# Hybrid conformer and state-space block on one core: time steps inside the exponentials, depthwise taps inside the scan, lower halves of the scan's weights by adding loads

## The chip, the core and the metric

The kernel runs on one NeuronCore of a Trainium2 chip. The metric is the device time of one execution in microseconds; the median of several runs counts. The engines are named as in the profile: PE (TensorE, matmuls), ACT (ScalarE), DVE (VectorE), POOL (GpSimd) and SP (SyncE, here only a queue for loads).

## The reference

One block on x of 512 tokens by 1024 channels, in float32:

```python
h = rms_norm(x, g);  proj = h @ w_in             # u_glu, z, xbc, dt_raw, gates
v = val * sigmoid(gt)                            # conformer branch
v = causal depthwise conv of 31 taps(v);  conv_out = silu(layer_norm(v)) @ pw_w + pw_b
xbc = silu(causal conv of 4 taps(xbc))           # state-space branch: xs, B, C
dt = softplus(dt_raw + dt_bias);  a_cs = cumsum(dt * -exp(a_log)) in each chunk
xdt = x * dt
y_diag = (C B^T * exp(a_cs[l] - a_cs[s]), causal) @ xdt
states = B^T @ (exp(a_cs[-1] - a_cs) * xdt);  carried from chunk to chunk
y = y_diag + exp(a_cs) * C @ prev + x * d_skip
ssm_out = grouped_rms_norm(y * silu(z)) * norm_g @ out_w
x = x + rms_norm((g_conv * conv_out + g_ssm * ssm_out) @ w_out)
x = x + rms_norm(silu-gated FFN(rms_norm(x)))    # hidden size 2816
```

The branch has 32 heads of 64 in 8 groups, with a state of 128 in each group. The kernel uses chunks of 128 tokens, so there are four.

## The kernel before

Every large product is made three times with operands in two halves: an operand is split into an upper half (`hi`, a cast to fp32r) and a lower half (`lo`, what the cast left out), and `mm3` (L241 to L252) issues hi by hi, hi by lo and lo by hi into one PSUM bank. PE therefore carries a dense row of matmuls from end to end, and everything else has to keep ahead of it.

The weights come in pieces of 128 x 1024 in a fixed list (`ORDER`, L147 on), numbered n. SP loads a piece into `raw` (L194), ACT casts it to `whi` (L202), and then there are two ways to the lower half. DVE subtracts `whi` from `raw` (L209); or ACT writes -whi into `wlo` (L206) and POOL issues a load of the same piece that adds to it (L207, an adding load). Before the change, in `w_part` (L195 to L211), pieces with an odd number above 8 and ahead of the `gc` gates go the second way, and even ones go to DVE. Five pieces have buffers at a time, and a piece is split up to three (`zz`: four) pieces ahead of its use, as soon as PE is done with the piece that had the buffer.

The stages are: the GLU projections (`val`, `glu`, pieces 0 to 18), with z of group 0 and dt in between; then the scan, groups 0 to 7 (pieces 19 to 76); then the gates `gs`, the last strips of the scan's output product and the gates `gc`; then the pointwise product, w_out and the FFN.

A group g of the scan projects x (two strips), B and C. Each strip is 24 matmuls into one bank, followed by a causal convolution of 4 taps (`conv4`, L596: one pass on ACT, three on DVE, a silu on ACT). Odd groups from 3 on also multiply an earlier pair of groups with the output weights (`so`), and even groups from 2 on project z for two groups at once (`zz`, four pieces that are used together, L634). In between stand the steps of the group before: `s1` (L656) transposes x, B and makes C B^T; `s2` (L689) makes the states (pS) and y_diag (yd); `s3` (L712) the part from the carried state (pY) and the norm; `s4` (L752) transposes y back. In `s1`, DVE reads each bank of transposed x twice, for `xdt` (times dt) and for `y` (times d_skip), and makes `xdec` out of xdt. `make_L` (L482) loads the running sums of a group to all partitions, masks them on POOL and takes 16 exponentials on ACT with `nacs` (minus the sums) as bias; DVE then multiplies L by C B^T (L686).

The 31-tap convolution of the conformer branch is 8 strips of one ACT pass and 30 DVE taps (L507 to L518). `conv_some` hands out taps in a fixed number: 12 per strip in the GLU stage, `TAPS[g]` in group g, `TAPS_GATE` behind each gate.

The order of instructions on each engine is fixed when the program is built: a scheduler places each instruction, in program order as far as its inputs are ready by its own estimates. Activations passed to `by_table` (L476) keep their order among each other, so that the activation table changes seldom.

Of the kernel before, what the change touches and what calls it, by code (L numbers as in the profile page):

```python
# [10 lines left out]
F32 = mybir.dt.float32  # L11
F32R = mybir.dt.float32r
BF16 = mybir.dt.bfloat16
AF = mybir.ActivationFunctionType
ALU = mybir.AluOpType
# [3 lines left out]
P = 128  # L19
T = 512  # L20
NT = T // P
# [4 lines left out]
HD = 64  # L26
G = 8
HG = H // G
# [49 lines left out]
LOAD_AT = {0: 0, 1: 1, 2: 2, 3: 4, 5: 6}  # L78
RAW_AHEAD = 3
EARLY_U = 4  # L80
DMA_EVERY = 2
DMA_FROM = 8
ADD_LO = (2, 3) + tuple(range(7, FF // P, 2))
GU_AHEAD = 5
# [1 line left out]
S_AHEAD = 5  # L86

TAPS_GLU = 12
TAPS = (6, 14, 18, 20, 20, 20, 20, 20)
TAPS_GATE = 5  # L90
ADD_S1 = (3, 5)
ORDER_DVE = (
# [72 lines left out]
def b3(ap, n):  # L165

    return ap.unsqueeze(len(ap.shape)).to_broadcast(list(ap.shape) + [n])
# [3 lines left out]
def block_kernel(ctx: ExitStack, tc: tile.TileContext, x, xT, x0, prm, hp, gp, wf, w, out):  # L171
    nc = tc.nc
    act, dve, pe, pool = nc.scalar, nc.vector, nc.tensor, nc.gpsimd
# [11 lines left out]
    seq = {key: n for n, key in enumerate(ORDER)}  # L185
# [10 lines left out]
    def w_part(n, c, by_dve=False):  # L196
        hi, lo = split[n]
        src = first_raw[n, c.start] if n < 3 else raws[n][:, c]
        if by_dve:
            dve.tensor_copy(hi[:, c], src)  # L200
        else:
            mark[n, c.start] = act.copy(hi[:, c], src)  # L202
        after_zz = n > 5 and ORDER[n - 2] in ZZ_LAST
        every = n % DMA_EVERY == DMA_EVERY - 1 and DMA_FROM < n < seq[("gc", 0)] and not after_zz
        if every or 0 <= n - seq[("wo", 0)] < ADD_WO:
            act.activation(lo[:, c], hi[:, c].bitcast(F32), AF.Copy, scale=-1.0)  # L206
            mark["lo"] = pool.dma_start(lo[:, c], w[n][:, c].bitcast(F32R), accum_op=ALU.add)  # L207
        else:
            mark["wlo"] = dve.tensor_tensor(out=lo[:, c], in0=src, in1=hi[:, c].bitcast(F32), op=ALU.subtract)  # L209
            if ORDER[n] == ZZ_LAST[0]:  # L210
                not_before(noted["yz_1"], mark["wlo"])  # L211
# [84 lines left out]
    ssd = br.enter_context(tc.tile_pool(name="ssd", bufs=1))  # L296
# [24 lines left out]
    def flat(a):  # L321
        return a.rearrange("p a b -> p (a b)")
# [9 lines left out]
    ps = aux_tile("warm_ps")  # L332
# [27 lines left out]
    hp_t = ssd.tile([P, 3, H], F32, name="hp_t")  # L360
# [97 lines left out]
    def running_sums():  # L458
        pcs = aux_tile("pcs")
        pe.matmul(pcs[:, :CH], tri, flat(ta), start=True, stop=True)  # L460
        act.copy(flat(acs), pcs[:, :CH])
        pend = aux_tile("pend")
        pe.matmul(pend[:, :CH], ones, flat(ta), start=True, stop=True)
        act.activation(flat(cd), pend[:, :CH], AF.Exp)
        act.activation(flat(eacs), flat(acs), AF.Exp)
        dve.tensor_tensor(out=flat(tb), in0=pend[:, :CH], in1=flat(acs), op=ALU.subtract)
        act.activation(flat(dec), flat(tb), AF.Exp)
        dve.tensor_scalar(out=flat(nacs), in0=flat(acs), scalar1=-1.0, scalar2=None, op0=ALU.mult)
        pT = aux_tile("pT")
        pe.transpose(pT[:, :P], flat(acs), ident)  # L470
        act.copy(acsT, pT[:, :P])
        for c in range(NT):
            nc.scalar.dma_start(scr[:, c, :], acsT[c * H : (c + 1) * H, :])


    def by_table(ins):  # L476

        if "table" in mark:
            not_before(ins, mark["table"])
        mark["table"] = ins  # L480
# [69 lines left out]
    for j in range(NK):  # L550
# [3 lines left out]
        if j == DT2:  # L554
            running_sums()
            L = {0: make_L(0)}
# [99 lines left out]
    def s1(g):  # L656
        s = st[g]
        hs = slice(HG * g, HG * (g + 1))
        xdt = ssd.tile([P, NT, HG, HD], F32, tag="xdt", name=f"xdt{g}")
        y = ssd.tile([P, NT, HG, HD], F32, tag="y", bufs=2, name=f"y{g}")  # L660
        xdec = ssd.tile([P, NT - 1, HG, HD], F32, tag="xdec", name=f"xdec{g}")
        for c2 in range(2):
            ps = aux_tile(f"pxT{g}_{c2}")
            for c in range(2):
                tok = slice((2 * c2 + c) * P, (2 * c2 + c + 1) * P)
                for e in range(2):
                    pe.transpose(ps[:, c * GW + e * P : c * GW + (e + 1) * P], s[f"x{e}"][:, tok], ident)
            cs = slice(2 * c2, 2 * c2 + 2)
            pv = ps.rearrange("p (c h d) -> p c h d", c=2, h=HG)
            dve.tensor_tensor(out=xdt[:, cs], in0=pv, in1=b3(dtt[:, cs, hs], HD), op=ALU.mult)  # L670
            dve.tensor_tensor(
                out=y[:, cs], in0=pv,
                in1=b3(hp_t[:, 2:3, hs].to_broadcast([P, 2, HG]), HD), op=ALU.mult,
            )
        dve.tensor_tensor(out=xdec, in0=xdt[:, : NT - 1], in1=b3(dec[:, : NT - 1, hs], HD), op=ALU.mult)
        ps = yd_tile(0, f"pBT{g}")
        for c in range(NT - 1):
            pe.transpose(ps[:, c * P : (c + 1) * P], s["B"][:, c * P : (c + 1) * P], ident)
        BT = ssd.tile([P, NT - 1, P], F32, tag="BT", name=f"BT{g}")
        act.copy(flat(BT), ps[:, : (NT - 1) * P])  # L680
        ps = yd_tile(1, f"pcb{g}")
        for c in range(NT):
            tok = slice(c * P, (c + 1) * P)
            pe.matmul(ps[:, tok], s["B"][:, tok], s["C"][:, tok], start=True, stop=True)
        L = s["L"].rearrange("p h c l -> p h (c l)")
        dve.tensor_tensor(out=L, in0=L, in1=ps.unsqueeze(1).to_broadcast([P, HG, T]), op=ALU.mult)  # L686
        s.update(xdt=xdt, y=y, xdec=xdec, BT=BT)

    def s2(g):  # L689
        s = st[g]  # L690
        hs = slice(HG * g, HG * (g + 1))
        prev = ssd.tile([P, NT - 1, HG, HD], F32, tag="prev", name=f"prev{g}")
        tmp = ssd.tile([P, HG, HD], F32, tag="ptmp", bufs=2, name=f"ptmp{g}")
        pa, pb = aux_tile(f"pSa{g}"), aux_tile(f"pSb{g}")
        pS = [pa[:, :GW], pa[:, GW:], pb[:, :GW]]
        for c in range(NT - 1):
            pe.matmul(pS[c], s["BT"][:, c, :], s["xdec"][:, c].rearrange("p h d -> p (h d)"), start=True, stop=True)
        act.copy(prev[:, 0].rearrange("p h d -> p (h d)"), pS[0])
        for c in range(1, NT - 1):
            dve.tensor_tensor(out=tmp, in0=prev[:, c - 1], in1=b3(cd[:, c, hs], HD), op=ALU.mult)  # L700
            dve.tensor_tensor(
                out=prev[:, c], in0=pS[c].rearrange("p (h d) -> p h d", h=HG), in1=tmp, op=ALU.add
            )
        yd = [yd_tile(n, f"yd{g}_{n}").rearrange("p (c h d) -> p c h d", c=2, h=HG) for n in range(2)]
        for c in range(NT):
            for h in range(HG):
                for i in range(0, P, HD):
                    half = slice(i, i + HD)
                    pe.matmul(yd[c // 2][half, c % 2, h, :], s["L"][:, h, c, half], s["xdt"][:, c, h, :], start=True, stop=True)
        s.update(prev=prev, yd=yd)  # L710

    def s3(g):  # L712
# [1090 lines left out]
```

## Time and profile before

| What | Value |
|---|---|
| median of 3 runs | 1017.67 us (1017.04 to 1017.77) |
| span of the profiled execution, first to last instruction | 1016.0 us |
| rest of the median around that span | 1.7 us |
| busy: PE, DVE, ACT, POOL | 1007.7, 847.9, 616.9, 106.7 us |
| moved by DMA | 155.02 MB |

The profile is of one execution and gives its span; the runs are timed apart from it, so the span is set beside their median. Busy time is summed by engine; a matmul's end is modelled, so that matmuls overlap in it, and short waits show better in the distances of their starts. In a group's line stand the source line, engine, operation, output and inputs, shapes and count, then busy time, the mean of one in ns, and the idle time ahead of it with what ended it. An arrow "<-" in brackets in a timeline names what a waiting instruction waited for.

### The profile page before, as it was taken

To read this page: it belongs to the slowest core of one execution; us is meant where nothing else is said; L and a number is where in the kernel's file an instruction comes from. 1 tells how busy PE (TensorE), PEld (TensorE's weight loads), DVE (VectorE), ACT (ScalarE), POOL (GpSimd) and SP (SyncE) were. 2 spreads that over 40 slices of the span, in tenths; PEclk is the share of its full clock that TensorE was granted. 3 is DMA by queue.
4 is the path that set the end of the run, shared out by engine and by line. 5 is a ranking of instruction groups with operands and counts; after the bars stand their busy time and mean duration, and the time that the engine had idled before them with its cause. 6 is when DMAs were issued, how large, how long until landed. Compare 5 with 4: busy or idle time off the path is not lost.

```text
span 1016.0 us, 15943 instructions
## 1 busy us (share of the span) xinstructions
PE 1007.7 (99%) x6184; PEld 881.7 (87%) x6184; DVE 847.9 (83%) x1233; ACT 616.9 (61%) x1038; POOL 106.7 (11%) x138
## 2 busy tenths in 40 slices
PE   9999999999999999999999999999999999999997
PEld 7898889888888888888888889889999999998886
DVE  7899977868696879678987889788999887899974
ACT  7655775667666746573552685466666566568552
POOL 0101202120121011100110111012000000001001
PEclk9999999999999999999999999999999999999999
DMA  8567635645554465356452355624755555469622
GB/s 302 151 168 218 158 96 145 187 110 144 158 151 117 130 182 151 102 135 163 99 139 69 114 142 165 223 104 118 230 151 160 153 143 146 128 177 295 212 83 83
DMA packets 43803, 155.02 MB, mean 153 GB/s; under 512 B 5072, under 2 KB 6096, under 8 KB 42704
## 3 DMA queue, kind: packets, MB, share of 16 engines
q1 hardware_dynamic: 30672, 105.44, 30.7%
q0 software_dynamic: 11136, 43.00, 21.7%
q10 hardware_dynamic: 1920, 5.57, 1.6%
q8 instruction: 48, 0.79, 0.3%
q14 instruction: 27, 0.22, 0.1%
HBM read 149.73 MB, written 4.26 MB: 152 GB/s over the span
## 4 chain that ended last, share of the span: by engine, by line
PE 87%; DVE 8%; ACT 3%; issue 1%; DMA 1%; SPq 0%; POOL 0%; POOLq 0%; DVEq 0%; ACTq 0%
PE xy L246 4%; PE xy L252 4%; PE xy L248 4%; PE pso L246 3%; PE pso L248 3%; PE pso L252 3%; PE yv L246 2%; PE yv L252 2%; PE yv L248 2%; PE px L246 2%; PE px L252 2%; PE px L248 2%; DVE a L514 2%; PE pz L248 2%; PE pz L252 2%; PE pz L246 2%
## 5 line engine op out<-in xcount | busy, mean ns | idle before, releaser
L514 DVE SCALAR_TENSOR_TENSOR a<-v,prm_t,a 128x511 f32<-128x511 f32 (+15 forms) x240 | 183.8, 769 | 14.3 <-ACT a L511 12.3
L202 ACT CAST whi<-raw 128x1024 fp32r<-128x1024 f32 x99 | 102.6, 1048 | 127.9 <-PE pso L248 36.7
L209 DVE TENSOR_TENSOR wlo<-raw,whi 128x1024 fp32r<-128x1024 f32 x58 | 70.6, 1220 | 32.7 <-ACT whi L202 32.5
L207 POOL DMA_DIRECT2D wlo<-in_w x41 | 36.5, 891 | 369.1 <-ACT wlo L206 171.4
L248 PE MATMUL pz<-wlo,hhi 128*128 128x512 f32 (+2 forms) x160 | 56.2, 351 | 0.2
L252 PE MATMUL pz<-whi,hlo 128*128 128x512 f32 (+2 forms) x160 | 56.1, 352 | 0.0
L246 PE MATMUL pz<-whi,hhi 128*128 128x512 f32 (+2 forms) x160 | 55.4, 353 | 0.0
L246 PE MATMUL px<-hhi,whi 128*128 128x512 f32 x128 | 50.2, 392 | 0.0
L246 PE MATMUL pso<-yh,whi 128*128 128x512 f32 x128 | 50.2, 394 | 0.0
L252 PE MATMUL px<-hhi,wlo 128*128 128x512 f32 x128 | 49.8, 389 | 0.0
L248 PE MATMUL px<-hlo,whi 128*128 128x512 f32 x128 | 49.8, 389 | 0.0
L248 PE MATMUL pso<-yl,whi 128*128 128x512 f32 x128 | 49.8, 390 | 0.0
L252 PE MATMUL pso<-yh,wlo 128*128 128x512 f32 x128 | 49.7, 390 | 0.0
L1189 ACT CAST whi_g<-raw 128x1024 fp32r<-128x1024 f32 x40 | 41.2, 1052 | 10.6 <-PE yv L248 4.9
L601 DVE SCALAR_TENSOR_TENSOR x<-px,prm_t,x 128x511 f32<-128x511 f32 (+2 forms) x48 | 34.7, 743 | 13.9 <-ACT x L599 13.8
L1196 DVE TENSOR_TENSOR wlo_g<-raw,whi_g 128x1024 fp32r<-128x1024 f32 x34 | 41.3, 1221 | 3.5 <-ACT whi_g L1189 3.4
L206 ACT ACTIVATE wlo<-whi 128x1024 fp32r<-128x1024 f32 x41 | 43.3, 1055 | 0.3
L496 ACT ACTIVATE L<-L,nacs 128x128 f32<-128x128 f32 x128 | 38.8, 389 | 0.1
L248 PEld LDWEIGHTS pz<-wlo,hhi 128*128 128x128 f32 x160 | 30.1, 188 | 4.9 <-DVE wlo L209 1.0
L246 PEld LDWEIGHTS pz<-whi,hhi 128*128 128x128 f32 x160 | 30.2, 189 | 3.9
L252 PEld LDWEIGHTS pz<-whi,hlo 128*128 128x128 f32 x160 | 30.1, 188 | 3.7
L1189 ACT CAST chi_g<-raw 128x1024 fp32r<-128x1024 f32 x24 | 24.9, 1053 | 8.8 <-PE yv L248 3.4
(763 smaller groups left out, 3450.7 us busy)
## 6 DMA issues: line engine op xcount, KB each, us to landing
raw<-in_w SPq DMA_DIRECT2D x182, 512.0 KB, 4.5
wlo<-in_w POOLq DMA_DIRECT2D x41, 512.0 KB, 6.8
L<-scr POOLq DMA_DIRECT2D x8, 1024.0 KB, 7.6
wlo_g<-in_w POOLq DMA_DIRECT2D x11, 512.0 KB, 7.0
clo_g<-in_w POOLq DMA_DIRECT2D x6, 512.0 KB, 5.5
pws<-in_w POOLq DMA_DIRECT2D x8, 256.0 KB, 5.9
pw_raws<-in_w SPq DMA_DIRECT2D x4, 512.0 KB, 7.0
xr<-in_x ACTq DMA_DIRECT2D x4, 512.0 KB, 3.9
```

Source lines behind the costliest of these rows:

```text
L202: mark[n, c.start] = act.copy(hi[:, c], src)
L206: act.activation(lo[:, c], hi[:, c].bitcast(F32), AF.Copy, scale=-1.0)
L207: mark["lo"] = pool.dma_start(lo[:, c], w[n][:, c].bitcast(F32R), accum_op=ALU.add)
L209: mark["wlo"] = dve.tensor_tensor(out=lo[:, c], in0=src, in1=hi[:, c].bitcast(F32), op=ALU.subtract)
L246: mark["pe"] = pe.matmul(ps, lh, rh, start=start, stop=False, skip_group_check=more)
L248: pe.matmul(ps, lh, rl, start=False, stop=False, skip_group_check=more)
L252: mark["pe3"] = pe.matmul(ps, ll, rh, start=False, stop=stop, skip_group_check=more)
L496: act.activation(L[:, h, c, :], L[:, h, c, :], AF.Exp, bias=nacs[:, c, HG * g + h : HG * g + h + 1])
L514: return dve.scalar_tensor_tensor(out=va[j][:, d:], in0=vs[j][:, : T - d], scalar=col("dw_w", j * KC + KC - 1 - d), in1=va[j][:, d:], op0= ...
L601: dve.scalar_tensor_tensor(out=a[:, d:], in0=ps[:, : T - d], scalar=col("ssm_w", i * KS + KS - 1 - d), in1=a[:, d:], op0=ALU.mult, op1=ALU ...
L1189: a_ = act.copy(hi, src)
L1196: d_ = dve.tensor_tensor(out=lo, in0=src, in1=hi.bitcast(F32), op=ALU.subtract)
```

## The change

Three things change. First, dt is no longer multiplied onto x. `running_sums` multiplies `dec` by dt, takes the logarithm of dt (not under 1e-38), and makes `nacs` the logarithm minus the sums, so that the exponentials of L bring dt with them. In `s1`, ACT copies each bank of transposed x to SBUF (`xt`, in the order of `by_table`), and DVE makes `xdec` and `y` from the copy. Second, the taps per group rise by 5 (group 0: 3), from 138 in all to 176, and the gates have none. Third, the adding loads take all pieces after number 19 up to the `gc` gates, but for 38, 54 and 70, the second ones after a z strip.

```diff
-TAPS = (6, 14, 18, 20, 20, 20, 20, 20)
-TAPS_GATE = 5
+TAPS = (9, 19, 23, 25, 25, 25, 25, 25)
+TAPS_GATE = 0
...
-        every = n % DMA_EVERY == DMA_EVERY - 1 and DMA_FROM < n < seq[("gc", 0)] and not after_zz
+        every = (n % 2 or n > seq["x", 0]) and DMA_FROM < n < seq[("gc", 0)] and not after_zz
...
-        dve.tensor_scalar(out=flat(nacs), in0=flat(acs), scalar1=-1.0, scalar2=None, op0=ALU.mult)
+        dve.tensor_tensor(out=flat(dec), in0=flat(dec), in1=flat(dtt), op=ALU.mult)
+        dve.tensor_scalar(out=flat(dtt), in0=flat(dtt), scalar1=1e-38, scalar2=None, op0=ALU.max)
+        act.activation(flat(dtt), flat(dtt), AF.Ln)
+        dve.tensor_tensor(out=flat(nacs), in0=flat(dtt), in1=flat(acs), op=ALU.subtract)
...
-            cs = slice(2 * c2, 2 * c2 + 2)
-            pv = ps.rearrange("p (c h d) -> p c h d", c=2, h=HG)
-            dve.tensor_tensor(out=xdt[:, cs], in0=pv, in1=b3(dtt[:, cs, hs], HD), op=ALU.mult)
-            dve.tensor_tensor(
-                out=y[:, cs], in0=pv,
-                in1=b3(hp_t[:, 2:3, hs].to_broadcast([P, 2, HG]), HD), op=ALU.mult,
-            )
-        dve.tensor_tensor(out=xdec, in0=xdt[:, : NT - 1], in1=b3(dec[:, : NT - 1, hs], HD), op=ALU.mult)
+            by_table(act.copy(xt[:, 2 * c2 : 2 * c2 + 2].rearrange("p c h d -> p (c h d)"), ps))
+        dve.tensor_tensor(out=xdec, in0=xt[:, : NT - 1], in1=b3(dec[:, : NT - 1, hs], HD), op=ALU.mult)
+        dve.tensor_tensor(out=y, in0=xt, in1=b3(hp_t[:, 2:3, hs].to_broadcast([P, NT, HG]), HD), op=ALU.mult)
...
-                    pe.matmul(yd[c // 2][half, c % 2, h, :], s["L"][:, h, c, half], s["xdt"][:, c, h, :], start=True, stop=True)
+                    pe.matmul(yd[c // 2][half, c % 2, h, :], s["L"][:, h, c, half], s["xt"][:, c, h, :], start=True, stop=True)
```

The order of instructions moves with it. On ACT in group 2, before: `whi_34` to `whi_37` are pieces of weights (33 to 36 are the four of the double z strip), `x2_0`, `x2_1`, `B2` strips of group 2, `pSa1` the states of group 1.

```order
L202 CAST whi_34_1798<-raw34_1684 128x1024
L605 ACT_TABLE_LOAD
L605 ACTIVATE x2_0_1714<-x2_0_1714 128x512
L605 ACTIVATE x2_1_1752<-x2_1_1752 128x512
L202 CAST whi_35_1901<-raw35_1721 128x1024
L599 ACTIVATE B2_1826<-pB2_1795,prm_t_75 128x512
L762 ACTIVATE yh0_1878<-pyT0_0_1880,prm_t_75 128x512
L202 CAST whi_36_1974<-raw36_1796 128x1024
L698 COPY prev1_1832<-pSa1_1834 128x256
L206 ACTIVATE wlo_35_1902<-whi_35_1901 128x1024
```

The same place on ACT in the changed kernel, where `xt1` is the copied x of group 1:

```order
L201 CAST whi_34_1816<-raw34_1701 128x1024
L201 CAST whi_35_1921<-raw35_1739 128x1024
L607 ACT_TABLE_LOAD
L607 ACTIVATE x2_0_1732<-x2_0_1732 128x512
L205 ACTIVATE wlo_34_1817<-whi_34_1816 128x1024
L205 ACTIVATE wlo_35_1922<-whi_35_1921 128x1024
L607 ACTIVATE x2_1_1770<-x2_1_1770 128x512
L670 COPY xt1_1776<-pxT1_0_1779 128x512
L670 COPY xt1_1776<-pxT1_1_1785 128x512
L601 ACTIVATE B2_1845<-pB2_1813,prm_t_75 128x512
L201 CAST whi_36_1995<-raw36_1814 128x1024
L205 ACTIVATE wlo_36_1996<-whi_36_1995 128x1024
```

The copies of x come in behind the second silu of x, two more lower halves (34, 36) are made here, and those of 34 and 35 stand ahead of that silu.

On PE at that place, before, from the end of B of group 2 (`pyT0_0` are transposes of group 0, `pC2` is C of group 2; of the six matmuls of C ahead of yd the first three are shown, the other three, which read the same, are left out):

```order
L761 MATMUL pyT0_0_1880<-ident_68,y0_1355 128x128 x4
L246 MATMUL pC2_1898<-hhi_79,whi_32_1686 128x512
L697 MATMUL pSa1_1834<-xdec1_1760,BT1_1780 128x256 x2
L697 MATMUL pSb1_1835<-xdec1_1760,BT1_1780 128x256
L248 MATMUL pC2_1898<-hlo_461,whi_32_1686 128x512
L252 MATMUL pC2_1898<-hhi_79,wlo_32_1687 128x512
L709 MATMUL yd1_0_1844<-xdt1_1758,L1_1256 64x64 x16
L709 MATMUL yd1_1_1845<-xdt1_1758,L1_1256 64x64 x16
```

On PE now, from the fifth matmul of C on:

```order
L247 MATMUL pC2_1918<-hlo_461,whi_32_1703 128x512
L251 MATMUL pC2_1918<-hhi_79,wlo_32_1704 128x512
L245 MATMUL pC2_1918<-hhi_79,whi_32_1703 128x512
L706 MATMUL yd1_0_1863<-xt1_1776,L1_1265 64x64 x16
L706 MATMUL yd1_1_1864<-xt1_1776,L1_1265 64x64 x11
L694 MATMUL pSa1_1853<-xdec1_1778,BT1_1797 128x256 x2
L694 MATMUL pSb1_1854<-xdec1_1778,BT1_1797 128x256
L706 MATMUL yd1_1_1864<-xt1_1776,L1_1265 64x64 x5
L758 MATMUL pyT0_0_1899<-ident_68,y0_1365 128x128 x4
```

yd moved ahead of the states and pyT0_0 behind them. Between the end of B and yd now stand seven matmuls of C and nothing else.

On POOL around the load of L for group 5, before (`rs2`, `rs3` are the norm factors of groups 2 and 3):

```order
L207 DMA wlo_49_2622<-in_w 128x1024
L258 TENSOR_SCALAR pm_2544<-ss2_2534 128x4
L259 TENSOR_TENSOR rs2_2535<-pm_2544,neg_half_73 128x4
L207 DMA wlo_51_2801<-in_w 128x1024
L486 DMA L5_3018<-scr_238 128x2048
L489 AFFINE_SELECT L5_3018<-L5_3018 128x2048
```

and now:

```order
L206 DMA wlo_50_2732<-in_w 128x1024
L206 DMA wlo_51_2837<-in_w 128x1024
L206 DMA wlo_52_2911<-in_w 128x1024
L488 DMA L5_3057<-scr_238 128x2048
L491 AFFINE_SELECT L5_3057<-L5_3057 128x2048
L206 DMA wlo_53_2918<-in_w 128x1024
L257 TENSOR_SCALAR pm_2893<-ss3_2883 128x4
L258 TENSOR_TENSOR rs3_2884<-pm_2893,neg_half_73 128x4
```

The issues of adding loads of 50 and 52 stand in POOL's row as well; the load of L and its mask stand behind that of 52.

More of the change, by code (lines that the diff above doesn't have):

```diff
@@ L80 @@
 EARLY_U = 4
-DMA_EVERY = 2
 DMA_FROM = 8
@@ L658, in s1 @@
         hs = slice(HG * g, HG * (g + 1))
-        xdt = ssd.tile([P, NT, HG, HD], F32, tag="xdt", name=f"xdt{g}")
+        xt = ssd.tile([P, NT, HG, HD], F32, tag="xdt", name=f"xt{g}")
         y = ssd.tile([P, NT, HG, HD], F32, tag="y", bufs=2, name=f"y{g}")
@@ L686, in s1 @@
         dve.tensor_tensor(out=L, in0=L, in1=ps.unsqueeze(1).to_broadcast([P, HG, T]), op=ALU.mult)
-        s.update(xdt=xdt, y=y, xdec=xdec, BT=BT)
+        s.update(xt=xt, y=y, xdec=xdec, BT=BT)
     def s2(g):
```

## The prediction

> **What bounds the kernel now.** I read the page's busy line first, then its chain of work, then the windows cut at the groups of the scan, then TensorE's own idle time. The page says that TensorE (PE) is busy for all but 8.3 us of the span, and that the chain is mostly PE's:
>
> ```profile
> span 1016.0 us, 15943 instructions
> PE 1007.7 (99%) x6184; PEld 881.7 (87%) x6184; DVE 847.9 (83%) x1233; ACT 616.9 (61%) x1038; POOL 106.7 (11%) x138
> PE 87%; DVE 8%; ACT 3%; issue 1%; DMA 1%; SPq 0%; POOL 0%; POOLq 0%; DVEq 0%; ACTq 0%
> ```
>
> The windows (columns: stretch, its length, then busy time and instruction count of PE, weight loads, DVE, ACT, POOL, the granted clock, DMA share, GB/s) give four of the eleven stretches from 108 to 603 us, in which everything lies that the change touches, and the sum of all eleven:
>
> ```profile
> 178.00:233.00 55.00, 54.95 (x312) 45.52 (x311) 39.52 (x53) 37.45 (x72) 8.30 (x9) 1.00 0.59 162
> 233.00:285.00 52.00, 51.63 (x297) 42.94 (x296) 42.13 (x59) 34.97 (x65) 7.23 (x8) 1.00 0.54 138
> 388.00:440.00 52.00, 51.85 (x297) 43.03 (x296) 35.10 (x49) 32.53 (x63) 7.41 (x8) 1.00 0.55 148
> 440.00:486.00 46.00, 46.00 (x272) 38.55 (x271) 42.84 (x63) 20.52 (x28) 3.46 (x4) 1.00 0.53 133
> sum 495.00, PE 494.43 PEld 413.01 DVE 396.78 ACT 299.61 POOL 61.48; mean PE 44.95 PEld 37.55 DVE 36.07 ACT 27.24 POOL 5.59
> ```
>
> PE is idle for 495.00 - 494.43 = 0.57 us of these 495 us, at granted clock 1.00. As many matmuls pass in 25 us when DVE is busy throughout and the DMA engines are full as when both are nearly idle, so their pace does not depend on the other engines:
>
> ```profile
> 925.00:950.00 25.00, 25.00 (x111) 20.57 (x110) 25.00 (x29) 17.93 (x25) 2.55 (x3) 1.00 1.02 315
> 975.00:1000.00 25.00, 25.00 (x111) 20.55 (x110) 11.95 (x17) 7.54 (x14) 1.30 (x4) 1.00 0.08 30
> ```
>
> The change takes no matmul away. So it can gain only where PE waits. Busy time hides part of a wait, so I read starts too (25 us / 111 = 0.225 us apart where nothing disturbs; the timeline's own steps are 0.227). Three places stand out in PE's timeline:
>
> ```profile
> 211.43 0.94 PE L248 MATMUL pz<-wlo,hhi 128*128 128x512 f32 x2
> 236.32 0.39 PE L248 MATMUL pB<-hlo,whi 128*128 128x512 f32 x1
> 237.08 0.66 PE L667 MATMUL pxT<-ident,x 128*128 128x128 f32 x4 [0.37 <-DVE yl L763]
> 418.97 0.39 PE L246 MATMUL pz<-whi,hhi 128*128 128x512 f32 x1
> 419.50 0.50 PE L248 MATMUL pz<-wlo,hhi 128*128 128x512 f32 x1
> ```
>
> Two matmuls should last 0.227 + 0.39 = 0.62, so 0.32 is lost at 211. From 236.32 to 237.08 is 0.76: 0.53 lost. From 418.97 to 419.50 is 0.53, and the second lasts 0.11 longer: 0.41 lost. Together 1.3 us. The first and the third stand at a weight's lower half with which DVE was late (at 210.61 in the rows below).
>
> **The change part by part.** Prices, from the groups and the timelines of the profile:
>
> ```profile
> L209 DVE TENSOR_TENSOR wlo<-raw,whi 128x1024 fp32r<-128x1024 f32 x58 | 70.6, 1220 | 32.7 <-ACT whi L202 32.5
> L206 ACT ACTIVATE wlo<-whi 128x1024 fp32r<-128x1024 f32 x41 | 43.3, 1055 | 0.3
> L207 POOL DMA_DIRECT2D wlo<-in_w x41 | 36.5, 891 | 369.1 <-ACT wlo L206 171.4
> q0 software_dynamic: 11136, 43.00, 21.7%
> DMA to landing us min/median/max: 5.5/6.8/10.0
> L514 DVE SCALAR_TENSOR_TENSOR a<-v,prm_t,a 128x511 f32<-128x511 f32 (+15 forms) x240 | 183.8, 769 | 14.3 <-ACT a L511 12.3
> L670 DVE TENSOR_TENSOR xdt<-pxT,dtt 128x512 f32<-128x512 f32 x16 | 10.9, 684 | 6.5 <-PE pxT L667 6.5
> L671 DVE TENSOR_TENSOR y<-pxT,hp_t 128x512 f32<-128x512 f32 x16 | 10.9, 682 | 0.0
> L740 DVE TENSOR_TENSOR y<-y,z 128x1024 f32<-128x1024 f32 x5 | 6.1, 1214 | 0.0
> L780 ACT COPY so<-pso 128x512 f32<-128x512 f32 x8 | 4.6, 577 | 2.9 <-PE pso L252 2.9
> 97.23 1.06 ACT L202 CAST whi<-raw 128x1024 fp32r<-128x1024 f32 x1 [4.38 <-PE pg L248]
> 210.61 1.21 DVE L209 TENSOR_TENSOR wlo<-raw,whi 128x1024 fp32r<-128x1024 f32 x1
> ```
>
> *Lower halves.* The adding loads go from 41 to 73. DVE loses 32 x 1.22 = 39 us, ACT gets 32 x 1.055 = 34 us, POOL 32 x 0.89 = 29 us. Queue 0 held the 16 DMA engines for 21.7% of 1016 = 220 us for 43.00 MB, so a load of 0.524 MB holds them for 2.7 us and 32 hold them for 86 us: the DMA share of the scan rises from about 0.55 to 0.72. None of this is on PE's path by itself. It takes away what caused the waits at 211 and 419: 0.7 us gained. Its cost is latency: a half that DVE had 1.22 us after ACT's cast now takes 1.06 on ACT and then 5.5 to 10.0 until it has landed.
>
> *Time steps.* Per group DVE gives up 2 x 0.684 + 2 x 0.682 and takes one product of 1024 elements out of SBUF, for which I take 1.21 (the L740 row, the nearest): 1.5 us less, 12 us in all. ACT takes two copies of 512 elements out of PSUM, 0.58 each by the L780 row, 9 us in all. Once, ahead of the scan, come two small DVE operations more and one small activation (Ln) with its table, under 2 us on ACT. ACT waits 4.38 us for PE right behind that place (97.23), which hides it; without that cover one weight's cast would come 2 us later. I cost it at nothing.
>
> *Taps.* 38 taps of 0.77 us move from the gates into the scan, 29 us. About six of the 32 halves belong to the gates' stretch, so DVE in the scan has -32 - 12 + 29 = -15 us, and the gates lose 29 and 7. The fullest stretch (42.84 of 46) gets no fuller: five taps more, 3.9 us, against four halves, 4.9, and 1.5. PE does not wait in the gates, so lighter gates gain nothing.
>
> *ACT's row.* At 37.45 of 55 and 32.53 of 52 ACT gets four or five halves and two copies, +6 us: under 44 of 55. But it works in order, and the copies now stand where section "The change" shows them: behind two casts, a table, two lower halves and two silus; behind them wait yd, xdec and pS of the group before, and B's first pass on ACT itself. Times of today in that place (group 2):
>
> ```profile
> 183.11 0.47 ACT L680 COPY BT<-pBT 128x384 f32<-128x384 f32 x1
> 184.19 1.04 ACT L202 CAST whi<-raw 128x1024 fp32r<-128x1024 f32 x1
> 185.25 1.28 ACT L605 ACT_TABLE_LOAD   x1
> 186.55 1.15 ACT L605 ACTIVATE x<-x 128x512 f32<-128x512 f32 x2
> 188.82 0.78 ACT L599 ACTIVATE B<-pB,prm_t 128x512 f32<-128x512 f32 x1 [0.18 <-PE pB L252]
> 188.34 2.28 DVE L686 TENSOR_TENSOR L<-L,pcb 128x2048 f32<-128x2048 f32 x1
> 188.62 0.60 PE L761 MATMUL pyT<-ident,y 128*128 128x128 f32 x4
> 191.83 2.08 PE L709 MATMUL yd<-xdt,L 128*64 128x64 f32 x64
> ```
>
> B's matmuls end at 188.62; seven of C behind them end at 190.2, where yd now wants its x. ACT from 183.11 + 0.47 = 183.6: two casts 2.1, the table 1.3, a silu 0.6, two halves 2.1, a silu 0.6, the first copy 0.6, makes 190.8. So yd waits 0.6. Against that, yd of today starts at 191.83 though L was ready at 188.34 + 2.28 = 190.62: the order has had up to 1.2 us to spare at such a place. Places of this kind are yd of groups 0, 1, 3 and 5 and pSb of group 7. Bounds: 0, or 5 x 1.2 = 6 us (0.6, and as much again where the order is further off). I take 0.15 each, 0.8 us, near the lower end, because all the places of today where PE was to go on just in time lose only the 0.53 at 236. That 0.53 goes as well: there a transpose waits for a bank that DVE frees, and it now stands six matmuls, 1.4 us, further back.
>
> *Sum.* Gained 0.7 + 0.5, lost 0.8, so 0.4 to 0.5 us less than the span of 1016.0. The median of the three runs is 1017.67, 1.7 above the span; that part I leave as it is. **1017.2 us.** About 0.2%, 2 us, is what a measurement of this kernel can tell from no change.
>
> **The rivals.** *Late halves (slower).* The last weight of each double z strip (36, 52, 68) had its half from DVE; now it is the last in ACT's row. Copies done 191.4, B's pass 0.8, cast 1.0, half 1.1: 194.3; landed 5.5 to 10.0 later, 199.8 to 204.3. PE wants it behind C's 24 matmuls from 188.62 (5.4), yd (2.1), pS and pY (three matmuls each, 1.3 by the chain's rows here), two times pyT (0.44) and 19 matmuls of z (4.3), at about 203.9:
>
> ```profile
> 300.43 0.44 PE pyT L761 x4
> 302.50 0.87 PE pYa L721 x4
> 303.36 0.43 PE pYb L721 x2
> ```
>
> It is late from a landing of 9.6 us on. With the loads doubled one more of 2.7 us can stand in front: 6.8 becomes 9.5 and 10.0 becomes 12.7, a wait of 0 to 3.1, in three groups 0 to 9.3 us; I price it at 4.5, with yd's waits 1021.7. For it speaks the longest landing of today; against it the median, which leaves 2.8 us. The Trainium skill's page DMA: Bandwidth & Descriptors (section Anatomy of one DMA — SWDGE (gpsimd) path) fits such a load as 2.0 us + bytes / 436e3; the estimate by it is 3.2 us for 512 KB, less than half of the median in this trace, and by it this rival would have no chance at all. *Copies in ACT's row (slower).* The waits of yd and pS come in at 0.6 in the five places and at half of that in the other three groups: 3.9 us on 1017.67 - 1.2, 1020.4. The working above speaks for it, the 1.2 us of spare time against it. *More than the waits (faster).* All 1.3 us gone and nothing lost gives 1016.4. Over 2 us needs PE to run closer in a way that the rows do not show; for it there is only the lighter DVE, against it the equal pace of the two rows of 111.
>
> **How the numbers follow.** Forecast (within 2 us) 0.65; late halves 0.10; copies 0.12; faster 0.13. The range begins at 1016.4, less 0.4 for the scatter of the runs (1017.04 to 1017.77) and 0.6 into the faster case, 1015.4, and ends in the copies' case at 1020.6; it leaves out the late halves and the far end of the faster case. Faster 0.13, same 0.65, slower 0.22.
>
> **What would show it.** Right: PE busy share as it is; no wait of PE at a lower half in the z strips; DVE's busy time down by about 50 us and ACT's up by about 44; idle of PE before yd and pS under 0.3 us each. Wrong: PE waiting a microsecond or more for ACT's copy (xt) or for a load into wlo; or none of this and yet a span 2 us shorter.

## The result, and the profile after

The changed kernel takes 1020.04 us (median of 9 runs, 1019.1 to 1020.73), the kernel before 1017.67: the ratio is 1.0025, interval 1.0015 to 1.0035. It is slower by 2.4 us, where 0.5 us less had been forecast; the time lies inside the forecast range, the sign is wrong. The profiled execution of the changed kernel took 1019.92 us with a span of 1018.1, against a span of 1016.0 before: 2.1 us more.

The page of the changed kernel shows first that the work moved as the change says (engines, queue 0, and the groups of the lower halves):

```profile
PE 1009.0 (99%) x6184; PEld 882.9 (87%) x6184; DVE 805.7 (79%) x1179; ACT 656.9 (65%) x1088; POOL 135.5 (13%) x170
q0 software_dynamic: 15744, 59.78, 30.6%
L205 ACT ACTIVATE wlo<-whi 128x1024 fp32r<-128x1024 f32 x73 | 76.6, 1058 | 0.7
L208 DVE TENSOR_TENSOR wlo<-raw,whi 128x1024 fp32r<-128x1024 f32 x26 | 31.6, 1220 | 25.2 <-ACT whi L201 25.2
```

DVE is busy 42 us less than before, ACT 40 and POOL 29 us more. PE executes the same 6184 matmuls and yet is busy 1.3 us longer. That is the first hint: part of the time goes where PE counts as busy, and no list of waits shows it. The waits that the trace does list for PE and that are new:

```profile
PE pSa L694 <- DVE xdec L671: 0.8, 2, 0.6
PE yd L706 <- ACT xt L670: 0.5, 1, 0.5
```

Total, number, longest: 1.3 us for the places that the prediction named. Against them, what before lost at the late lower halves (211 and 419 us) and at pxT's wait for its bank (236 us), 1.3 us by the starts, is gone. Waits gone and waits new are about equal, so the 2.1 us need another part.

To find it I take the start of the same matmul in both timelines, counted from the first x strip, and write down by how much the changed kernel is behind:

| where in PE's order | us behind |
|---|---|
| first x strip of group 2 (166 us of before's matmuls) | 0.58 |
| x of group 3 (218) | 0.84 |
| first `ssm_out` strip (238) | 0.30 |
| B of group 4 (283) | 0.28 |
| x of group 5 (321) | 1.91 |
| C of group 5 (355) | 1.53 |
| B of group 6 (386) | 1.56 |
| x of group 7 (425) | 1.58 |
| gates (476) | 1.66 |
| `ssm_out` of the last pair (518), and the end | 2.11 |

The times in brackets count from the first matmul that uses the inputs, at 4.35 us of the span. The losses stand exactly at the blocks of small matmuls (yd, pS, pyT) of groups 0, 1, 3, 5 and 7; the gains stand at the places where before waited, and in group 4. What such a block costs is the time from the start of the last large matmul ahead of it to the start of the first one behind it. In the kernel before, group 3 (start, duration, engine, line, operation):

```profile
292.25 0.40 PE L252 MATMUL pB<-hhi,wlo 128*128 128x512 f32 x1
292.48 1.03 PE L697 MATMUL pSa<-xdec,BT 128*128 128x256 f32 x4
293.35 0.59 PE L697 MATMUL pSb<-xdec,BT 128*128 128x256 f32 x2
293.87 2.08 PE L709 MATMUL yd<-xdt,L 128*64 128x64 f32 x64
295.89 0.65 PE L761 MATMUL pyT<-ident,y 128*128 128x128 f32 x4
296.30 0.48 PE L246 MATMUL pC<-hhi,whi 128*128 128x512 f32 x1
```

4.05 us, from 292.25 to 296.30. In the changed kernel, group 5, the same matmuls:

```profile
398.01 0.39 PE L245 MATMUL pC<-hhi,whi 128*128 128x512 f32 x1
398.33 1.73 PE L706 MATMUL yd<-xt,L 128*64 128x64 f32 x50
400.05 1.13 PE L694 MATMUL pSa<-xdec,BT 128*128 128x256 f32 x4
401.01 0.59 PE L694 MATMUL pSb<-xdec,BT 128*128 128x256 f32 x2
401.54 0.68 PE L706 MATMUL yd<-xt,L 128*64 128x64 f32 x14
402.15 0.66 PE L758 MATMUL pyT<-ident,y 128*128 128x128 f32 x4
402.56 0.48 PE L247 MATMUL pC<-hlo,whi 128*128 128x512 f32 x1
```

From 398.01 to 402.56 it is 4.55: 0.50 us more, with no wait listed in any row. The difference is the order: yd begins, pS comes after 50 of its 64 matmuls, then yd goes on. The first yd now starts 0.32 behind a large matmul (0.23 is the pace), the first pS takes 1.13 instead of 1.03 for its four, and the two pieces of yd need 1.73 + 0.68 where 64 in one needed 2.08. In group 3 the same order meets real waits as well:

```profile
294.59 0.39 PE L251 MATMUL pC<-hhi,wlo 128*128 128x512 f32 x1
295.45 1.73 PE L706 MATMUL yd<-xt,L 128*64 128x64 f32 x50 [0.47 <-ACT xt L670]
297.76 1.13 PE L694 MATMUL pSa<-xdec,BT 128*128 128x256 f32 x4 [0.58 <-DVE xdec L671]
298.73 0.59 PE L694 MATMUL pSb<-xdec,BT 128*128 128x256 f32 x2
299.26 0.68 PE L706 MATMUL yd<-xt,L 128*64 128x64 f32 x14
300.28 0.48 PE L245 MATMUL pC<-hhi,whi 128*128 128x512 f32 x1
```

5.69 us, 1.64 more than 4.05: 1.05 waited for, and 0.59 without a listed wait, close to the 0.50 of group 5. By the same reckoning group 0 is 0.59 longer (0.18 of it waited for xdec), group 1 0.66 (0.21 of it, since yd starts 0.53 instead of 0.32 behind the large matmul), and group 7 loses 0.45 by the table. Sum 3.84: 1.44 of waits and 2.4 of a split yd in five places. Gained are 0.54 at pxT, 0.75 at the two late halves, and 0.38 in group 4, together 1.7. 3.84 - 1.7 = 2.1, the 2.1 of the span.

Why the copies are late in group 3 stands in the rows of ACT and of DVE there:

```profile
292.75 1.06 ACT L201 CAST whi<-raw 128x1024 fp32r<-128x1024 f32 x1 [1.01 <-PE pB L247]
294.30 0.63 ACT L607 ACTIVATE x<-x 128x512 f32<-128x512 f32 x1 [0.49 <-DVE x L603]
294.83 1.06 ACT L670 COPY xt<-pxT 128x512 f32<-128x512 f32 x2
```

```profile
290.03 2.28 DVE L683 TENSOR_TENSOR L<-L,pcb 128x2048 f32<-128x2048 f32 x1
292.23 0.74 DVE L603 SCALAR_TENSOR_TENSOR x<-px,prm_t,x 128x510 f32<-128x510 f32 x1
293.52 0.74 DVE L603 SCALAR_TENSOR_TENSOR x<-px,prm_t,x 128x509 f32<-128x509 f32 x1
294.18 2.66 DVE L516 SCALAR_TENSOR_TENSOR a<-v,prm_t,a 128x484 f32<-128x484 f32 x4
296.76 0.95 DVE L671 TENSOR_TENSOR xdec<-xt,dec 128x768 f32<-128x768 f32 x1
```

ACT is not short of time there, it is idle: its silu waits for DVE's last tap of the second x strip, which waits behind the product of L and pcb (2.28 us). The copies end at 295.9, and xdec starts only at 296.76, behind four taps of the 31-tap convolution.

The price of a cut yd had stood in the profile of before too, in group 4, where two strips of `ssm_out` stood between:

```profile
351.62 1.96 PE L709 MATMUL yd<-xdt,L 128*64 128x64 f32 x58
359.18 0.45 PE L709 MATMUL yd<-xdt,L 128*64 128x64 f32 x6
```

58 matmuls take 1.96 and six take 0.45: 2.41 where 64 in one piece take 2.08. In the changed kernel yd of group 4 is in one piece, which fits the 0.38 gained there.

### The profile page after: what moved, and what is told of

The parts are those of the page before. It is cut to its first block, busy times and chain, and to the rows that moved or that the text cites. A ratio compares the mean times of both kernels' runs of the same rounds, so it can differ in the third digit from the quotient of the medians.

```text
span 1018.1 us, 15982 instructions
## 1 busy us (share of the span) xinstructions
PE 1009.0 (99%) x6184; PEld 882.9 (87%) x6184; DVE 805.7 (79%) x1179; ACT 656.9 (65%) x1088; POOL 135.5 (13%) x170
## 4 chain that ended last, share of the span: by engine, by line
PE 83%; ACT 6%; DVE 4%; issue 4%; POOL 1%; DMA 1%; POOLq 0%; DVEq 0%; ACTq 0%; SPq 0%
PE xy L245 4%; PE xy L251 4%; PE xy L247 4%; PE pz L245 3%; PE pz L251 3%; PE pz L247 3%; PE pso L247 2%; PE pso L251 2%; PE pso L245 2%; PE yv L245 2%; PE yv L247 2%; PE yv L251 2%; PE px L247 2%; PE px L245 2%; PE px L251 2%
## 5 line engine op out<-in xcount | busy, mean ns | idle before, releaser
L516 DVE SCALAR_TENSOR_TENSOR a<-v,prm_t,a 128x485 f32<-128x485 f32 (+16 forms) x240 | 182.4, 763 | 5.8 <-ACT a L513 2.4
L206 POOL DMA_DIRECT2D wlo<-in_w x73 | 64.2, 879 | 338.9 <-ACT wlo L205 205.5
L205 ACT ACTIVATE wlo<-whi 128x1024 fp32r<-128x1024 f32 x73 | 76.6, 1058 | 0.7
L208 DVE TENSOR_TENSOR wlo<-raw,whi 128x1024 fp32r<-128x1024 f32 x26 | 31.6, 1220 | 25.2 <-ACT whi L201 25.2
```

The source lines that it names most:

```text
L516: return dve.scalar_tensor_tensor(out=va[j][:, d:], in0=vs[j][:, : T - d], scalar=col("dw_w", j * KC + KC - 1 - d), in1=va[j][:, d:], op0= ...
```

## The experiments

Theory A, formed from the list of waits: PE reaches yd and pS before xt and xdec are made. Rival B: the adding loads cost the time. Rival C: the taps make DVE late. A2, formed after e1: part of the loss is the split of yd by pS, part is waits. All runs in one table; the last column is how far the end of PE's work lies behind that of before, counted from the first x strip, in one profiled execution each. The kernel before was run again with each set of experiments, on another chip than the set ahead of it, so runs of different sets are compared by their distance from before. The ratio with its interval is not exactly the quotient of the two medians.

| run | median us | before, same runs | ratio, 95% interval | behind in the profile |
|---|---|---|---|---|
| e1 held | 1019.59 | 1017.40 | 1.0019, 1.0010 to 1.0028 | 2.1 |
| e2 no folding | 1019.63 | 1017.40 | 1.0020, 1.0011 to 1.0029 | 4.2 |
| e3 folding only | 1020.46 | 1017.40 | 1.0026, 1.0015 to 1.0037 | 3.0 |
| e4 no loads | 1021.49 | 1017.40 | 1.0038, 1.0024 to 1.0052 | 4.1 |
| e5 unsplit | 1018.84 | 1017.34 | 1.0014, 1.0005 to 1.0023 | 1.4 |
| e6 held all | 1018.26 | 1017.34 | 1.0012, 1.0003 to 1.0021 | 0.7 |
| e7 split before | 1020.36 | 1017.34 | 1.0029, 1.0016 to 1.0041 | 3.8 (2.7 at the end of the scan) |
| e8 loads only | 1019.47 | 1017.34 | 1.0022, 1.0013 to 1.0031 | 1.4 |
| e9 product later | 1018.35 | 1017.54 | 1.0006, 0.9997 to 1.0015 | 0.8 |
| e10 copies on DVE | 1018.36 | 1017.54 | 1.0008, 0.9999 to 1.0017 | 1.1 |
| e11 DVE, held | 1017.70 | 1017.54 | 1.0001, 0.9992 to 1.0010 | -0.2 |
| e12 taps only | 1019.94 | 1017.54 | 1.0023, 1.0013 to 1.0034 | 2.1 |
| e13 as e11, 12 | 1017.77 | 1017.53 | 1.0004, 0.9995 to 1.0013 | 0.0 |
| e14 folding, held | 1017.47 | 1017.53 | 1.0003, 0.9994 to 1.0012 | -0.5 |
| e15 loads, held | 1019.08 | 1017.53 | 1.0018, 1.0009 to 1.0028 | 1.5 |

**e1: the block held back.**

```diff
     def proj_bc(g, n, between=None):
...
+        proj(ps, wt, ks=slice(0, 6))
+        if between:
+            with tc.issue_after(mark["pe3"].ins):
+                s2(between - 1)
+        proj(ps, wt, ks=slice(6, NK))
```

`between` is given for C of groups 1, 2, 4 and 6 (`s2` of groups 0, 1, 3, 5); `s2` of group 7 goes into the third strip of gates in the same way. `issue_after` puts PE's instructions of the block behind the matmul named.

> The changed kernel with one thing altered: in groups 0, 1, 3, 5 and 7 the small matmuls yd, pSa and pSb are held back behind 18 of the 24 matmuls of the strip C (12 of the third strip of gates for group 7); they stood behind 10, 7, 9, 4 and 0 of them. All work is there. Theory A (the 2 us were lost because TensorE's order brings yd and pS to the places where the copies xt and the product xdec are only just or not yet made): the waits of about 0.6, 0.65, 1.6, 0.5 and 0.55 us, 3.9 together, go away and nothing takes their place, so about 1016.1 us. Rival B (the 32 more adding loads cost the time, by ScalarE's row, GpSimd or the DMA traffic): nothing is changed in them, so 1020.0 as before the edit. Rival C (five taps more of VectorE in each group make all that hangs on VectorE late): later yd does not help the chain on VectorE, so 1019 to 1020.

1019.59, not 1016.1: 2.2 us above before, where the changed kernel is 2.4 above. The waits of yd are gone, but this one stands in their place:

```profile
PE pyT L763 <- ACT xt L675: 1.8, 2, 1.3
```

pyT takes its banks in turn with pxT, and the bank that comes next still holds x for the copy. So the copies are late for PE wherever it first meets them; ACT's row in group 1 shows what stands ahead of them:

```profile
188.56 1.99 ACT L205 ACTIVATE wlo<-whi 128x1024 fp32r<-128x1024 f32 x2
190.45 0.61 ACT L607 ACTIVATE x<-x 128x512 f32<-128x512 f32 x1
190.97 1.05 ACT L675 COPY xt<-pxT 128x512 f32<-128x512 f32 x2
```

Two lower halves. That supports the waits of theory A. But group 1's block, for which no wait is listed, was still 0.45 us longer than in one piece (pSb stood two matmuls ahead of the end of yd), so A had to be changed into A2.

**e2: without the folding** (the `s1` and `running_sums` of before, loads and taps of the changed kernel).

> The changed kernel without the folded time steps: xdt and y come out of PSUM by VectorE as before, the adding loads and the taps stay as changed. Theory A: the copies on ScalarE are gone and with them the five waits; the waits at the late lower halves at 211 and 419 us stay away, the wait of pxT for a bank (0.5 us) comes back: 1017.67 - 0.7 = 1017.0 us. Rival B: 1020, since all the loads are there. Rival C: 1020, since all the taps are there.

1019.63, near the 1020 of B and C and not A's 1017.0: the folding is not the only cause. The profiled execution (1021.86 us, the slowest of its eleven runs) shows one loss at 206 us, here in PE's timeline and in the windows (from, to; length, busy us of PE, PEld, DVE, ACT and POOL; granted clock; DMA share, GB/s):

```profile
206.14 0.69 PE L248 MATMUL pz<-wlo,hhi 128*128 128x512 f32 x1 [1.81 <-DMA wlo<-in_w]
206.63 0.63 PE L252 MATMUL pz<-whi,hlo 128*128 128x512 f32 x1
209.19 0.63 PE L252 MATMUL pz<-whi,hlo 128*128 128x512 f32 x1
```

```profile
206.00:210.00 4.00, 3.86 (x10) 3.05 (x11) 4.00 (x8) 0.39 (x1) 0.75 (x1) 0.57 0.23 93
```

The adding load of the last of the four z weights, issued at 194.99, was there at 206.1, 1.8 us after PE wanted it, and behind that wait the granted clock was 0.57 in a window of 4 us; from 206.63 to 209.19 seven matmuls start, 0.43 us apart instead of 0.23. This is the rival "late halves" of the prediction: 11.1 us where the limit had been put at 9.6. The median, 2.2 us below this execution, says that it is not so long in most runs.

**e3: the folding alone** (lower halves and taps of before).

> The kernel before with the folded time steps alone: copies xt on ScalarE, xdec and y out of SBUF; lower halves and taps as they were. Theory A: the copies stand in ScalarE's row as in the changed kernel, with one lower half less in front of them: waits of 0.3 to 1.6 us in the five places, 2 to 3.5 us together, less 0.5 for the wait of pxT, so 1019.2 to 1020.7 us. Rival B: 1017.2 us, the wait of pxT gone and nothing else. Rival C: 1017.2 us as well.

1020.46, inside A's range; B and C alone would have given 1017.2. In the profile pS stands inside yd in groups 0, 1, 3 and 5, and at these blocks one wait is listed, in group 1:

```profile
PE yd L706 <- ACT xt L670: 1.0, 1, 1.0
```

**e4: folding and taps, lower halves of before.**

> The changed kernel with the lower halves as before (41 adding loads, every second weight by VectorE), folding and taps as changed. Theory A: the copies are made as late as in e3 or a little later on VectorE's side, 1019.2 to 1021 us. Rival B: 1017 us, since the loads that cost the time are gone. Rival C: as in the changed kernel or slower, 1020 to 1022, since VectorE has taps and halves both.

1021.49, more than with the loads: that the loads are the cause of the whole is out. The time lies above A's range (1019.2 to 1021) and inside C's (1020 to 1022), so the taps as a part of the cause stand. pS stands inside yd in groups 0, 1, 3, 5 and 7, and the waits are elsewhere once more, at places that hang on DVE:

```profile
PE pYa L718 <- DVE prev L698: 0.9, 1, 0.9
PE pxT L669 <- DVE yl L760: 0.7, 2, 0.4
```

**e5: yd behind pSb, nothing else.**

```diff
-            pe.matmul(pS[c], s["BT"][:, c, :], s["xdec"][:, c].rearrange("p h d -> p (h d)"), start=True, stop=True)
+            last = pe.matmul(pS[c], s["BT"][:, c, :], s["xdec"][:, c].rearrange("p h d -> p (h d)"), start=True, stop=True)
...
-        for c in range(NT):
+        with tc.issue_after(last.ins):
+            for c in range(NT):
...
```

> The changed kernel with one rule more for TensorE's order: the 64 matmuls of yd stand behind pSb in every group, so that pS no longer stands inside yd; the scheduler then puts the block later by itself (behind 16, 14, 15 and 10 matmuls of the strip C in groups 0, 1, 3, 5). All work is there. Theory A2 (of what the changed kernel loses at its five places, 0.44 us each is what it costs TensorE to go from yd to pS and back in the middle of yd, 2.2 in all, and about 1.6 are waits for xt and xdec in groups 0, 1 and 3): both go, 1020.0 - 3.8 = 1016.2 us. Theory A as it stood before e1 (only waits, moved elsewhere by a bank when one moves the block): the waits go to another place, 1019 to 1020. Rivals B (adding loads) and C (taps): 1020.

1018.84, 1.5 us above before, where the changed kernel is 2.4 above: 0.9 us less, of 3.8 expected, and the two intervals overlap. The splits are gone from the timeline; the waits are again at pyT:

```profile
PE pyT L759 <- ACT xt L670: 1.4, 2, 0.9
```

**e6: unsplit, block and pyT held.**

> As e5, and in groups 0, 1, 3, 5 and 7 the block of pS and yd held behind 18 matmuls of the strip C (12 of the third strip of gates), and the transposes pyT of the group before held behind that block, which in e1 waited 1.8 us for a bank that the copy xt had to free. Theory A2: nothing of the copies is left on TensorE's path, 1016.2 us, as e5 or a little less. Rival D (what e1 lost was not the bank and the switches but the later block itself: prev, pY and the gates of z come later): 1018 to 1020.

1018.26, 0.9 us above before: 1.5 less than the changed kernel's 2.4, but 2 above what A2 said. No split is left; what is listed is xdec itself, in groups 1 and 3, although the block stands behind 18 matmuls:

```profile
PE pSa L701 <- DVE xdec L678: 1.0, 2, 0.7
```

**e7: the split alone, put into the kernel before.**

```diff
+        for c in range(2):
...
+                    last = pe.matmul(yd[c // 2][half, c % 2, h, :], s["L"][:, h, c, half], s["xdt"][:, c, h, :], start=True, stop=True)
+        with tc.issue_after(last.ins):
+            for c in range(NT - 1):
+                last = pe.matmul(pS[c], s["BT"][:, c, :], s["xdec"][:, c].rearrange("p h d -> p (h d)"), start=True, stop=True)
...
+        with tc.issue_after(last.ins):
+            for c in range(2, NT):
...
```

> The kernel before with one thing altered: in all eight groups the block is issued as half of yd, pSa, pSb, other half of yd. No work is added or taken. Theory A2: eight times 0.44 us of switching between the small tiles of yd and the full ones of pS, 3.5 us, so about 1021 us; TensorE's intervals at the switches show it with nothing waited for. Theory A (only waits): 1017.4 to 1018, since yd waits for nothing new.

1020.36, 3.0 us more than before, from the order alone. Group 3 of it, to be read against the same group of before above (4.05 us):

```profile
292.58 0.39 PE L252 MATMUL pB<-hhi,wlo 128*128 128x512 f32 x1
292.89 1.15 PE L701 MATMUL yd<-xdt,L 128*64 128x64 f32 x32
293.98 1.13 PE L704 MATMUL pSa<-xdec,BT 128*128 128x256 f32 x4
294.94 0.59 PE L704 MATMUL pSb<-xdec,BT 128*128 128x256 f32 x2
295.47 1.15 PE L716 MATMUL yd<-xdt,L 128*64 128x64 f32 x32
296.55 0.66 PE L768 MATMUL pyT<-ident,y 128*128 128x128 f32 x4
296.96 0.48 PE L246 MATMUL pC<-hhi,whi 128*128 128x512 f32 x1
```

4.38 us, 0.33 more, and nothing waited for; 0.44 had been expected. Six of the other groups lose 0.33 to 0.36 in the same way, and group 2, whose yd is cut a second time by matmuls of `ssm_out`, loses 0.75: 3.2 us in all. PE is 2.7 behind at the end of the scan, less than 3.2 in the main because the late halves of before cost less when PE comes later. (The rest of the 3.8 in the table comes from 877 to 904 us, in the feed-forward part, where matmuls of 256 columns start 0.118 instead of 0.113 us apart in this one execution; why is open.) The split as a cost of its own is shown. The Trainium skill's page TensorEngine Tiling (Array Packing), section Key Properties, says that a change of tiling mode drains TensorE; these rows agree, at 0.33 us for the cut.

**e8: the loads alone.**

> The kernel before with the 32 more adding loads alone. Theory A2: the waits at the late halves at 211 and 419 us go and nothing else changes: 1016.7 to 1017.0 us, unless a lower half is late, as it was once in e2 (1.8 us at 206 us, with slower matmuls for 3.4 us behind it). Rival B, that the loads cost: 1019 to 1020 us, with waits for the loads of lower halves in the strips z.

1019.47: as B said, but not by the waits for loads that B named. No wait for a load is listed; PE's order now has pS of group 1 directly behind B, ahead of its product:

```profile
PE pSa L697 <- DVE xdec L675: 1.2, 1, 1.2
```

**e9: e6 with the product of L behind the x taps** (a `not_before` edge from the product to the last of these taps).

> As e6, and VectorE takes the product of L and pcb (2.28 us) only behind the three taps of the second x strip; in e6 it stood between them, so that ScalarE waited for these taps in groups 3 and 5 (idle 0.5 to 1.8 us) before it could make the copies xt. Theory E (in group 3 it is VectorE's row, and not ScalarE's, that makes the copies late; in group 1 it is ScalarE's two lower halves in front): of e6's waits of pSa for xdec, 0.4 us in group 1 and 0.8 in group 3, that of group 3 goes and that of group 1 stays: 1018.26 - 0.8 = 1017.5 us. Rival F: the product is now late itself and yd waits for it: 1018.3 us or more.

1018.35, 0.8 us above before where e6 was 0.9 above: no gain, where 0.8 had been expected. xdec is in time now in both groups, so moving this one instruction of DVE was enough in group 1 too, which theory E had put down to ACT. But PE now waits for DVE one step later, because `prev` stands among the taps and holds the bank of pS:

```profile
PE pyT L769 <- DVE prev L708: 2.0, 2, 1.1
```

**e10: as e5, the copies by DVE.**

```diff
-            by_table(act.copy(xt[:, 2 * c2 : 2 * c2 + 2].rearrange("p c h d -> p (c h d)"), ps))
+            dve.tensor_copy(xt[:, 2 * c2 : 2 * c2 + 2].rearrange("p c h d -> p (c h d)"), ps)
```

> As e5, with the two copies xt of each group on VectorE in place of ScalarE (0.68 us each by the rows of before). Theory E: ScalarE's row no longer stands ahead of yd, pS and pyT; the 1.4 us for which pyT waited for xt in e5 go: about 1017.4 us; the block is put up to 16 matmuls earlier again by the scheduler, and a wait of pSa for xdec of up to 1 us may come in group 1 as in e8: 1017.2 to 1018.4. Rival C (VectorE's row is the cause): VectorE has 11 us more and the waits grow: 1019 to 1020.

1018.36, at the upper end of theory E's range; C's 1019 to 1020 is missed. No wait for xt is left, one of 0.7 us for the product L is new.

**e11: e9 and e10 together.**

> e9 and e10 together: block held behind 18 matmuls, no split, product behind the taps, copies on VectorE. If the places of yd, pS and pyT are all that the folding costs, nothing of it is left, and the waits at the late halves of before are gone: 1016.3 us, faster than both kernels. If the later block costs by itself (prev, pY, z's products), 1018.

1017.70 against 1017.54: the same time as before, not 1016.3. One wait of the scan is left, with switches beside it, 1 us in all (the other 0.4 follows at the end of this section):

```profile
PE pyT L769 <- ACT whi L201: 0.5, 1, 0.5
```

**e12: the taps alone** (`TAPS` and `TAPS_GATE` of the changed kernel).

> The kernel before with the taps alone moved from the gates into the scan (38 of them). Theory A2: TensorE's order keeps pS in front of yd and its distance behind the strip B within three matmuls of before, so 1017.0 to 1017.8 us. Rival C (the taps make VectorE late in the scan): 1018.5 us or more, with waits for xdec, L or lower halves of weights.

1019.94: C's range, and one of the waits that C named, a lower half that DVE makes too late in the strip z of group 6:

```profile
PE pz L248 <- DVE wlo L209: 1.4, 1, 1.4
```

In the changed kernel this half comes by an adding load, so the wait is not there; this harm of the taps hangs on halves that stay on DVE. The rest of the loss stands at yd of groups 6 and 7, which this order cuts.

**e13, e14, e15: what each part does once the order is mended.** e13 is e11 with 12 matmuls instead of 18; e14 is e11 with the lower halves and taps of before; e15 is e8 with the block held behind 12 matmuls in groups 0 and 1 (and 12 of gs 2 in group 7) and yd behind pSb.

> As e11, the block held behind 12 instead of 18 matmuls of the strip C (1.4 us earlier). In e11 one place still lost: the second pyT in group 3's strip z waited 0.7 us for a bank and 0.25 us went in switches beside it, both because the block came so late. If the copies on VectorE leave room enough, that goes and nothing comes: 1016.8 us. If 12 is too early, waits of pSa for xdec come in groups 1 or 3: 1017.7 to 1018.5.

> e11 without the adding loads and without the taps: the folding alone, with the block held, unsplit, and the copies on VectorE. Against e3 (folding alone, 1020.46) this shows what of its 3 us was TensorE's order: if all of it, 1017 us, with waits at the late lower halves of VectorE at about 211 and 419 us (0.7) left and the wait of pxT gone. If the folding has another price, 1018.5 or more.

> The kernel before with the 32 more adding loads alone (e8: 1019.47), its block of pS and yd behind 12 matmuls of C in groups 0 and 1, which was in e8 one matmul behind B or less, and yd behind pSb everywhere. If what e8 lost was that place (pSa waited 1.2 us for xdec) and small ones like it, 1017.0 to 1017.5 us; if the loads cost by their traffic, 1019 or more.

e13 came out at 1017.77, like e11; the wait of pyT for ACT's cast is still there, so 12 or 18 is not what makes it. e14 came out at 1017.47, against e3's 1020.46: the 3 us of the folding alone are gone with order, copies and product moved; which of the three gave how much was not taken apart. e15 came out at 1019.08, missing its 1017.0 to 1017.5 and at the number that was to speak for the loads' traffic. The block is in time now, but pyT waits for the bank that `prev` holds:

```profile
PE pyT L769 <- DVE prev L708: 0.9, 1, 0.9
```

That again is no wait for a load, and the traffic as a cause is not shown. But `ssm_out` waits 0.4 us for a product of ACT here (0.3 in e8), whose row the added halves lengthen, so not all of rival B is excluded.

The fifteen timelines show one thing more. Strips of `ssm_out` cut yd of group 6 in e2, e3, e4, e8, e10 to e13 and e15, with or without the folding. From B of group 7 to the gates, where that block stands, PE falls behind by another 0.4 to 1.0 us in these nine runs, and by 0.1 at most in the changed kernel, e1, e5, e6, e9 and e14, where it is whole. In e11 it is 0.4. In e12 it is 0.7, and pSb cuts group 7 for 0.4 more.

None of the fifteen is faster than the kernel before by more than the interval.

## Why the prediction was wrong, point by point

- *What bounds the kernel, and what there is to gain*: right. PE is the bound; what was lost at 211, 236 and 419 us is gone, 1.3 us against the 1.2 counted. No wait for a lower half stands in the z strips, as forecast.
- *Engines' time, time steps once, taps in the gates*: right. DVE -42 (forecast -50), ACT +40 (44). The extra work ahead of the scan cost nothing that the profile shows: counted from the first matmul that uses the inputs, the first x strip starts 0.02 us earlier than before.
- *The five places where yd and pS come in just in time*: **the step that failed**, "I take 0.15 each, 0.8 us, near the lower end". The places were the right ones, groups 0, 1, 3, 5 and 7; they cost 3.84 us. Two things were missed. The first is in no bound: the new order lets pS cut yd in two, and I moved the block with the duration that it had, although PE's new order in "The change" shows the cut. Five cuts cost 2.4 us by the place-by-place sum. e7 shows 0.33 to 0.36 per cut with no wait at all, which makes 1.7 of it; why the changed kernel's cuts cost 0.1 more each is not shown. The second is the waits, 1.44 us where 0.8 was counted; they lie within the bounds of 0 to 6. ACT's row was read rightly where the working was made, in group 1: yd starts at 191.1 and its x had been put at 190.8. But most of the waiting is in group 3 (0.47 for xt and 0.58 for xdec, where under 0.3 each was the sign of being right), and there the copies and xdec wait for DVE's taps and product, which the working left out.
- *The spare time as an argument*: that every place of today loses little was read as a property of the kernel. It is one of the order that stood there. e3, e8 and e12 show that each part alone makes the scheduler write another order, and that each of these kernels loses 2 to 3 us, with waits or cuts in places where before had none.
- *Rival "copies in ACT's row"* (1020.4) gave the time, and its places in the main; of its mechanism only the waits are shown, a bit over a third of the loss, so that its number is close is luck in good part. *Rival "late halves"*: no wait for a load stands in the changed kernel's profile, and one in e2's. *"Faster"*: nothing for it.
- The gain in group 4 (0.38, yd in one piece there) was not foreseen either. That the time lies inside the range is luck too: the range's upper end came from waits alone.

What stays open: how often an adding load lands late, since each trace is of one execution, what more the added loads cost through ACT's row, and whether the folding with a mended order is faster by a few tenths, which intervals of 0.9 us either way cannot tell.

## What to carry to other kernels

When a change moves a block of small matmuls, look in the new order not only at where it stands but at whether it is still in one piece: here, cutting 64 small-tile matmuls by six full-tile ones costs 0.33 to 0.5 us, in busy time, where no list of waits shows it. On an engine that is 99% busy, a change worth a microsecond must be judged together with the order that the scheduler writes for it: the folding alone lost 3 us (e3), and nothing that could be measured with the block held and whole, the copies on DVE and the product later (e14). Moving a late consumer later does not remove the wait if the same buffer has another user: e1, e5, e9 and e15 each met it again at a bank.

## What the hardware showed that I had not expected

- A cut of a run of 128x64 matmuls by 128x256 ones costs 0.33 us (e7) to 0.50 us (group 5 of the changed kernel) without any wait.
- After PE had waited 1.81 us for a load (e2), the granted clock was 0.57 for the next 4 us and matmuls started 0.43 instead of 0.23 us apart, so the wait cost about twice its length. After waits of 1.40 us (e12) and 1.1 us (e9) the clock stayed at 1.00.
